# Seven block products in place of eight in the ConvFFN up-projections of a two-layer encoder step

## Chip, cores and metric

The kernel runs on one core of one Trainium2 chip. The metric is the device time of one execution in microseconds. TensorE multiplies, VectorE (DVE) and ScalarE (ACT) do elementwise work, GpSimd (POOL) too, and SyncE (SP) issues most DMAs.

## What is computed

One inference step of a trunk of two layers over 1088 tokens of width 1024 in fp32: 1024 tokens of a prompt and 64 of a sample stream. Layer 0 mixes tokens by pooling, layer 1 by a gated linear recurrence (HGRN2); behind each mixer stands a ConvFFN, which the change is about:

```python
def conv_ffn(h, hist, w_up, cw, cb, w_down):          # h: [L, 1024], D_FF = 2816
    up = jnp.einsum('bld,df->blf', h, w_up)           # [L, 2 * 2816]
    gate_pre, val = jnp.split(up, 2, axis=-1)
    ext = jnp.concatenate([hist, gate_pre], axis=1)
    conv = cb
    for j in range(3):
        conv = conv + cw[j] * ext[:, j:j + L]         # causal, along the tokens
    hid = jax.nn.silu(conv) * val
    y = jnp.einsum('blf,fd->bld', hid, w_down)
    return y, ext[:, -2:]

x += mixer(rmsnorm(x)); x += conv_ffn(rmsnorm(x))     # per layer; a last rmsnorm behind both
```

## The kernel before

Activations lie with features on partitions and tokens along the free axis, in three chunks: chunk 0 and 1 of 384 prompt tokens, chunk 2 of 256 prompt and 64 sample tokens, 320 columns (`CH`, `NCOL`). The residual `x` and the normalised activations stay in SBUF. An fp32 product is made of three fp32r matmuls: each operand is split into a high part and the rest (`hnhi`, `hnlo` for activations, `whi`, `wlo` for weights), and `mm3` (L121-125) adds high x high, high x low and low x high.

Weights are streamed. A unit is 128 x 1024: a DMA on SP brings it as `raw` (L102), ScalarE casts it to `whi` (L103), GpSimd subtracts to `wlo` in two halves (L106). There are six places for units (`NW`); `drop` says which have no more use, and `load_ready` then writes the next loads of `queue`. The pooling weights `pw` are units 0 and 1.

A ConvFFN has 22 feature tiles j in 11 groups of two. `up` (L441) makes for a tile and a chunk the gate `pg` and the value `pv`, each of eight k-tiles x 3 = 24 matmuls; ScalarE copies the gate to `ge` (L466) and starts the convolution (L480), VectorE makes its other two steps (L481, L482), ScalarE the silu (L483), VectorE the product `hr` with the value (L485), and `split` makes `hh` (L128, ScalarE) and `hl` (L129, VectorE). The last two columns of a gate go to the next chunk by small copies on GpSimd (`carry`, L465, L468), those of chunk 2 to an output (`ncv`, L475, L476). `down` (L495) makes for each of eight column blocks d a `dn` of six matmuls per chunk and adds it to `x` (L501).

Ahead of each ConvFFN `norm` makes sums of squares (L260, L261), a transposing matmul `nps` (L272), the root on VectorE, another transposing matmul `nr` (L285), and then scales the eight k-tiles (L300) and splits them.

TensorE's order is written ahead of time: each piece is a `Task`, a generator with a priority and delays (`L_HID`, `N_SUM`, ...) behind other tasks, and `run` takes at each planned time the ready task of the lowest priority; where none is ready in the first 130 us it writes small `fill` matmuls (L178). Up parts have rising priorities from 1000, a `down` has 500, pooling and norms come first. The other engines' order comes from the scheduler. In group 0 and in the last one the chunks are the outer loop, in the others the tiles.

Of the kernel before, what the change touches and what calls it, by code (L numbers as in the profile page):

```python
# [43 lines left out]
NW = 6  # L44
# [12 lines left out]
def trunk_kernel(ctx: ExitStack, tc: tile.TileContext, xtok, xs_tok, hist_tok, xf, par, gmix, pw, winm, ident_in,  # L57
# [24 lines left out]
    queue = []  # L82
    loaded = {}

    def q_add(key, src):
# [4 lines left out]
    def load_ready(most=None):  # L90
        """Loads the next units whose place in the ring is free."""
        while queue and (len(order) < NW or order[-NW] in dead) and (most is None or len(order) < most):
            key, src = queue.pop(0)
            i = len(order)
            order.append(key)
            hi = wp.tile([P, D], F32R, name=f"whi{i}", tag="whi")
            lo = wp.tile([P, D], F32R, name=f"wlo{i}", tag="wlo")
            if i in (1, 3, 5):
                raw = sp.tile([P, D], F32, name=f"raw{i}", tag="raw2")
            else:  # L100
                raw = rawp.tile([P, D], F32, name=f"raw{i}", tag="raw")
            nc.sync.dma_start(raw, src)  # L102
            nc.scalar.copy(hi, raw)  # L103
            for o in range(0, D, D // 2):
                cs = slice(o, o + D // 2)
                nc.gpsimd.tensor_tensor(lo[:, cs], raw[:, cs], hi[:, cs].bitcast(F32), op=ALU.subtract)  # L106
# [803 lines left out]
```

## Time and profile before

| | us |
| --- | --- |
| time, median of 3 runs | 2384.64 |
| lowest, highest | 2383.80, 2385.51 |
| span of the profiled execution | 2382.1 |
| TensorE busy in it | 2329.7 |
| VectorE busy | 1277.3 |
| ScalarE busy | 744.8 |
| GpSimd busy | 668.5 |
| ConvFFN of layer 0, about | 100 to 880 |
| HGRN2, about | 880 to 1560 |
| ConvFFN of layer 1, about | 1560 to 2360 |

The span is that of one profiled execution, from its first to its last instruction. Its own time isn't listed beside it; the runs' times lie 1.7 to 3.4 us above the span, and the median 2.5. A matmul's record lasts longer than the distance to the next one, since they are pipelined; the pace is read from the starts.

### The profile page before, as it was taken

The page shows a single profiled execution, that of the slowest core. Times are in us where ns is not written, and L with a number is a line of the kernel's source. Part 1 is how long each engine was busy: PE and PEld are TensorE (multiplying, and loading weights), DVE is VectorE, ACT ScalarE, POOL GpSimd, SP SyncE. Part 2 cuts the span into 40 slices and gives each one's busy share as a digit, 9 for nine tenths or more (in the row PEclk, how much of TensorE's full clock was granted, in tenths as well). Part 3 has the DMA queues.
Part 4 walks back from the last instruction along what each step waited for, and adds up shares of the span by engine and source line. Part 5 has one row for each costly group of instructions (what it writes and reads, how often), then busy time and mean ns, then how long its engine had stood idle before and what let it go on. Part 6 is the DMA issues. An engine that isn't in the chain of part 4 may idle for free.

```text
span 2382.1 us, 35919 instructions
## 1 busy us (share of the span) xinstructions
PE 2329.7 (98%) x14260; PEld 2286.0 (96%) x14260; DVE 1277.3 (54%) x3242; ACT 744.8 (31%) x1502; POOL 668.5 (28%) x842
## 2 busy tenths in 40 slices
PE   9999999999999989999999999989999999999997
PEld 8999999999999989998998998989999999999997
DVE  6834343344443488677667667774443344443446
ACT  5532222322222353323323323343222322222224
POOL 3232222322232252112112112253232322232324
PEclk8999999999999999999999999999999999999999
DMA  7111111111111110001001001001111111111101
GB/s 242 31 54 41 49 45 45 54 36 45 45 45 45 36 55 27 22 31 54 22 22 55 21 31 49 27 23 52 45 45 45 54 41 40 45 45 45 54 27 77
DMA packets 33811, 111.06 MB, mean 47 GB/s; under 512 B 4061, under 2 KB 8029, under 8 KB 33258
## 3 DMA queue, kind: packets, MB, share of 16 engines
q1 hardware_dynamic: 33582, 108.64, 13.7%
q8 instruction: 112, 1.84, 0.3%
q14 instruction: 57, 0.47, 0.1%
q10 hardware_dynamic: 60, 0.12, 0.0%
HBM read 103.03 MB, written 5.72 MB: 46 GB/s over the span
## 4 chain that ended last, share of the span: by engine, by line
PE 87%; DVE 8%; DMA 1%; ACT 1%; POOL 1%; issue 1%; SPq 0%; DVEq 0%; ACTq 0%; POOLq 0%
PE pg L123 7%; PE pg L125 7%; PE pg L124 7%; PE pv L123 7%; PE pv L124 7%; PE pv L125 7%; PE dn L125 7%; PE dn L124 7%; PE dn L123 7%; PE pj L123 4%; PE pj L124 4%; PE pj L125 4%; PE pl L674 3%; DVE q L665 1%; PE op L123 1%; PE op L124 1%
## 5 line engine op out<-in xcount | busy, mean ns | idle before, releaser
L106 POOL TENSOR_TENSOR wlo<-raw,whi 128x512 fp32r<-128x512 f32 x348 | 474.9, 1381 | 1064.2 <-ACT whi L103 1056.3
L501 DVE TENSOR_TENSOR x<-x,dn 128x384 f32<-128x384 f32 (+1 forms) x528 | 279.8, 531 | 239.0 <-PE dn L125 237.2
L123 PE MATMUL dn<-hh,whi 128*128 128x384 f32 (+1 forms) x1056 | 345.1, 327 | 1.9 <-DVE x L501 1.3
L125 PE MATMUL dn<-hh,wlo 128*128 128x384 f32 (+1 forms) x1056 | 344.5, 326 | 0.7 <-POOL wlo L106 0.7
L124 PE MATMUL dn<-hl,whi 128*128 128x384 f32 (+1 forms) x1056 | 344.6, 326 | 0.6 <-DVE hl L129 0.6
L123 PE MATMUL pv<-hnhi,whi 128*128 128x384 f32 (+1 forms) x1056 | 344.8, 327 | 0.0
L123 PE MATMUL pg<-hnhi,whi 128*128 128x384 f32 (+1 forms) x1056 | 344.7, 326 | 0.0
L124 PE MATMUL pv<-hnlo,whi 128*128 128x384 f32 (+1 forms) x1056 | 344.3, 326 | 0.0
L125 PE MATMUL pg<-hnhi,wlo 128*128 128x384 f32 (+1 forms) x1056 | 344.2, 326 | 0.0
L125 PE MATMUL pv<-hnhi,wlo 128*128 128x384 f32 (+1 forms) x1056 | 344.2, 326 | 0.0
L124 PE MATMUL pg<-hnlo,whi 128*128 128x384 f32 (+1 forms) x1056 | 343.9, 326 | 0.0
L481 DVE SCALAR_TENSOR_TENSOR cv<-ge,prm,cv 128x384 f32<-128x384 f32 x132 | 83.5, 633 | 479.7 <-ACT cv L480 469.4
L103 ACT CAST whi<-raw 128x1024 fp32r<-128x1024 f32 x174 | 182.6, 1049 | 494.1 <-PE dn L124 123.7
L123 PE MATMUL pj<-hnhi,whi 128*128 128x384 f32 (+1 forms) x768 | 269.9, 351 | 0.0
L125 PE MATMUL pj<-hnhi,wlo 128*128 128x384 f32 (+1 forms) x768 | 252.6, 329 | 0.0
L124 PE MATMUL pj<-hnlo,whi 128*128 128x384 f32 (+1 forms) x768 | 252.1, 328 | 0.0
L123 PEld LDWEIGHTS dn<-hh,whi 128*128 128x128 f32 x1056 | 198.2, 188 | 3.7 <-DVE x L501 2.4
L125 PEld LDWEIGHTS dn<-hh,wlo 128*128 128x128 f32 x1056 | 198.2, 188 | 1.1 <-POOL wlo L106 1.1
L124 PEld LDWEIGHTS dn<-hl,whi 128*128 128x128 f32 x1056 | 198.1, 188 | 0.8 <-DVE hl L129 0.8
L123 PEld LDWEIGHTS pv<-hnhi,whi 128*128 128x128 f32 x1056 | 198.4, 188 | 0.1
L123 PEld LDWEIGHTS pg<-hnhi,whi 128*128 128x128 f32 x1056 | 198.2, 188 | 0.1
L124 PEld LDWEIGHTS pv<-hnlo,whi 128*128 128x128 f32 x1056 | 198.4, 188 | 0.0
(238 smaller groups left out, 3792.7 us busy)
## 6 DMA issues: line engine op xcount, KB each, us to landing
raw<-w_up_in SPq DMA_DIRECT2D x88, 512.0 KB, 3.2
raw<-w_dn_in SPq DMA_DIRECT2D x44, 512.0 KB, 3.2
raw<-w_in_in SPq DMA_DIRECT2D x32, 512.0 KB, 3.2
raw<-w_out_in SPq DMA_DIRECT2D x8, 512.0 KB, 3.2
xt<-xtok_in SPq DMA_DIRECT2D x7, 448.0 KB, 6.1
x<-xf_in SPq DMA_DIRECT2D x2, 1536.0 KB, 9.3
y_out<-x SPq DMA_DIRECT2D x8, 384.0 KB, 2.3
x<-xf_in SPq DMA_DIRECT2D x1, 1280.0 KB, 8.2
```

What stands on the lines that cost most here:

```text
L103: nc.scalar.copy(hi, raw)
L106: nc.gpsimd.tensor_tensor(lo[:, cs], raw[:, cs], hi[:, cs].bitcast(F32), op=ALU.subtract)
L123: nc.tensor.matmul(ps, w[0][:, wsl], a_hi, start=first, stop=False)
L124: nc.tensor.matmul(ps, w[0][:, wsl], a_lo, start=False, stop=False)
L125: nc.tensor.matmul(ps, w[1][:, wsl], a_hi, start=False, stop=last)
L481: nc.vector.scalar_tensor_tensor(t[:, :wd], ge[:, 0:wd], prm[:, cw[0]:cw[0] + 1], t[:, :wd], op0=ALU.mult, op1=ALU.add)
L501: nc.vector.tensor_tensor(x[c][:, d, :], x[c][:, d, :], pd[:, :n], op=ALU.add)
L665: nc.vector.tensor_tensor(dst, src, fac, op=ALU.mult)
L674: nc.tensor.matmul(pls[-1][:w, i % 2 * MW:i % 2 * MW + 3 * w // 2], kk[:, o:o + w], mv, start=True, stop=True)
```

## The change

For ten of the eleven groups of each ConvFFN, the gate and value of a feature tile over chunks 0 and 1 are taken as one product of 2 x 2 blocks: the weight blocks a11, a12 (gate, k-tiles 0-3 and 4-7), a21, a22 (value) and the activation blocks b11, b21 (chunk 0, k-tiles 0-3 and 4-7), b12, b22 (chunk 1). Strassen's scheme makes it of seven block products of 12 matmuls instead of eight. Product 1 is (a11+a22)(b11+b22), 2 (a21+a22) b11, 3 a11 (b12-b22), 4 a22 (b21-b11), 5 (a11+a12) b22, 6 (a21-a11)(b11+b12), 7 (a12-a22)(b21+b22). Products 3 and 5 are added up in one bank (`px`, the gate of chunk 1), 4 and 2 in another (`py`, the value of chunk 0); `e` holds 1+3+4, from which the other two results come by VectorE and GpSimd (`part`, L653).

- **Sums of activations.** `sums` (L403) makes the five right-hand sums: sum 1 in a new tile (`mix..1`), sums 4 and 3 in place in `hn` of chunk 0 and chunk 1 (`sum..4k`, `sum..3k`, for k 0-3), 7 and 6 in new tiles. Each of the four k-steps is three VectorE operations (L419, L420, L421), a cast on ScalarE and a subtraction on GpSimd (L169); for 7 and 6 every second L420 is on GpSimd. Group 0 is computed plainly, chunk after chunk, while they are made; sum 4 waits for chunk 0's last use in it and sum 3 for chunk 1's.
- **Weights.** The unit is a half, 128 x 512, in eight places (four more in the HGRN2 part), with five `raw` buffers. `q_mix` (L128) loads a block or, for products 1, 2, 5, 6 and 7, two blocks that VectorE adds or subtracts (L134) ahead of the cast.
- **Order.** A group is: products 3, 4, 1, 5 of its first tile and chunk 2 plainly, the `down` of the group before (chunks inside the column block; `L_HID` 8.5), products 2, 7, 6, then the second tile. In group 1 product 4 stands first. In the last group chunk 2 is computed at the end, from blocks that are loaded again. The plain part starts the convolution behind `pg`, ahead of `pv`.
- The work tiles of norms, HGRN2 and ConvFFN share buffers in another way, and two delays of the norm ahead of HGRN2 are longer.

The instructions on TensorE go from 13538 matmuls to 13079, 66 and 87 of which are `fill`; on VectorE from 3242 to 3714, on GpSimd from 842 to 1138, SP's DMAs from 236 to 818.

```diff
-NW = 6
+NR, NR_G = 8, 4
+NRAW = 5
...
+            hi = pool.tile([P, HW_], F32R, name=f"whi{nm}", tag=f"whi{i}", bufs=1)
+            lo = pool.tile([P, HW_], F32R, name=f"wlo{nm}", tag=f"wlo{i}", bufs=1)
+            src = make(nm)
+            nc.scalar.copy(hi, src)
+            nc.gpsimd.tensor_tensor(lo, src, hi.bitcast(F32), op=ALU.subtract)
...
+    PARTS = {"a11": (0,), "a12": (1,), "a21": (2,), "a22": (3,), "a5": (0, 1, ALU.add), "a2": (2, 3, ALU.add),
+             "a1": (0, 3, ALU.add), "a7": (1, 3, ALU.subtract), "a6": (2, 0, ALU.subtract)}
...
+            t = [raw_block(f"{nm}_{b}", (gate, val)[b // 2], b % 2) for b in bs[:2]]
+            if len(t) > 1:
+                nc.vector.tensor_tensor(t[0], t[0], t[1], op=bs[2])
...
+    def sums(l, ts, after, used=None):
...
+        while used and used.done is None:
+            yield 0.0, 1.0
+        n = [0]
+        for t in ts:
+            op = ALU.subtract if t in "43" else ALU.add
+            (ah, al), (bh, bl) = {"1": (quarter[0], quarter[3]), "4": (quarter[2], quarter[0]), "3": (quarter[1], quarter[3]),
+                                  "7": (mix["4"], mix["1"]), "6": (mix["3"], mix["1"])}[t]
+            for k in range(4):
...
+                with tc.issue_after(after()):
+                    nc.vector.tensor_tensor(m, ah[:, k, :].bitcast(F32), bh[:, k, :].bitcast(F32), op=op)
+                    (nc.gpsimd if t in "76" and k % 2 else nc.vector).tensor_tensor(r, al[:, k, :].bitcast(F32), bl[:, k, :].bitcast(F32), op=op)
+                    nc.vector.tensor_tensor(m, m, r, op=ALU.add)
+                    split(mix[t][0][:, k, :], mix[t][1][:, k, :], m, nc.gpsimd)
+                yield 0.0, L_MIX[t in "76"]
...
+        def prod(ps, key, t, first=True):
...
+            for k in range(4):
+                mm3(ps[:, :N0], get(key), slice(k * P, k * P + P), mix[t][0][:, k, :], mix[t][1][:, k, :], first and k == 0, k == 3, not first)
...
+                if t in "341":
+                    if hasattr(self, "e"):
+                        nc.vector.tensor_tensor(self.e, self.e, ps[:, :N0], op=ALU.add)
+                    else:
+                        self.e = kept(f"e{nm}", "e", 2, ps)
...
+                elif t == "7":
+                    g0 = slot(f"g{nm}", "g", 1)[:, :N0]
+                    nc.gpsimd.tensor_tensor(g0, self.e, self.ge1[:, 2:2 + N0], op=ALU.subtract)
...
+                    nc.gpsimd.tensor_tensor(self.e, self.e, self.v0, op=ALU.subtract)
+                    nc.vector.tensor_tensor(ge0[:, 2:2 + N0], g0, ps[:, :N0], op=ALU.add)
...
+                b0, b1 = (Block(j, jj, hid) for jj, j in enumerate(js))
+                a = task(lambda b=b0, end=end, gi=gi: up_a(b, end, "34"[gi == 1]), prev)
+                Task(lambda f=before: down(*f), 500, [(prev, L_HID), (a, 0.0)])
+                prev = task(lambda b=b0, end=end: up_b(b, end), a)
```

TensorE at the start, layer 0. `pg0_1_0` is the gate of feature tile 1 over chunk 0, `nr_f01` the second transposing matmul of chunk 1's norm. Before:

```order
L124 MATMUL pv0_0_0_668<-hnlo0_103,whi3_297 128x384
L125 MATMUL pv0_0_0_668<-hnhi0_100,wlo3_298 128x384
L123 MATMUL pg0_1_0_775<-hnhi0_100,whi4_304 128x384
L124 MATMUL pg0_1_0_775<-hnlo0_103,whi4_304 128x384
L125 MATMUL pg0_1_0_775<-hnhi0_100,wlo4_305 128x384
L123 MATMUL pg0_1_0_775<-hnhi0_100,whi4_304 128x384
L124 MATMUL pg0_1_0_775<-hnlo0_103,whi4_304 128x384
L125 MATMUL pg0_1_0_775<-hnhi0_100,wlo4_305 128x384
L123 MATMUL pg0_1_0_775<-hnhi0_100,whi4_304 128x384
L124 MATMUL pg0_1_0_775<-hnlo0_103,whi4_304 128x384
L125 MATMUL pg0_1_0_775<-hnhi0_100,wlo4_305 128x384
L285 MATMUL nr_f01_786<-ident_88,nt_f01_700 128x128 x3
```

And now, where `pd2_0` is the first matmul of chunk 2's pooling:

```order
L165 MATMUL pv0_0_0_670<-hnhi0_97,wloup_0_0_a22_315 128x384
L242 MATMUL fill_779<-warm_86 128x128 x2
L242 MATMUL fill_782<-warm_86 128x128 x2
L242 MATMUL fill_785<-warm_86 128x128
L382 MATMUL nr_f01_787<-ident_85,nt_f01_711 128x128 x3
L242 MATMUL fill_795<-warm_86 128x128
L242 MATMUL fill_801<-warm_86 128x128 x2
L242 MATMUL fill_808<-warm_86 128x128 x2
L242 MATMUL fill_815<-warm_86 128x128
L242 MATMUL fill_817<-warm_86 128x128
L242 MATMUL fill_823<-warm_86 128x128
L242 MATMUL fill_825<-warm_86 128x128
```

The matmuls of tile 1 over chunk 0 stood around `nr_f01` and ahead of chunk 2's pooling; now they stand behind chunk 2's pooling mix, and single `fill` matmuls, 21 up to `pd2_0`, are in their place.

GpSimd at the end of group 0 in layer 0: `wlo8` to `wlo10` are low parts of units 8 to 10, two halves each, and `ncv0` the output of the convolution's last columns. Before:

```order
L106 TENSOR_TENSOR wlo8_1370<-raw8_1371,whi8_1369 128x512
L475 COPY ncv0_95<-ge0_0_2_1350 128x2
L476 COPY ncv0_95<-ge0_0_2_1350 128x2
L106 TENSOR_TENSOR wlo8_1370<-raw8_1371,whi8_1369 128x512
L463 MEMSET ge0_2_0_1658 128x2
L106 TENSOR_TENSOR wlo9_1377<-raw9_1378,whi9_1376 128x512 x2
L106 TENSOR_TENSOR wlo10_1517<-raw10_1518,whi10_1516 128x512
L475 COPY ncv0_95<-ge0_1_2_1497 128x2
L476 COPY ncv0_95<-ge0_1_2_1497 128x2
L106 TENSOR_TENSOR wlo10_1517<-raw10_1518,whi10_1516 128x512
```

And now, with `hnlo0` and `hnlo1` the low parts of sums 4 and 3, and `wloup` and `wlodn` those of a weight half of group 1's up and group 0's down part:

```order
L169 TENSOR_TENSOR hnlo0_100<-sum042_1387,hnhi0_97 128x384
L169 TENSOR_TENSOR hnlo0_100<-sum043_1415,hnhi0_97 128x384
L111 TENSOR_TENSOR wloup_0_2_a12_1469<-rawup_0_2_a12_1_1470,whiup_0_2_a12_1468 128x512
L111 TENSOR_TENSOR wloup_0_2_a21_1494<-rawup_0_2_a21_2_1495,whiup_0_2_a21_1493 128x512
L169 TENSOR_TENSOR hnlo1_101<-sum030_1452,hnhi1_98 128x384
L580 COPY ncv0_92<-ge0_1_2_1499 128x2
L581 COPY ncv0_92<-ge0_1_2_1499 128x2
L111 TENSOR_TENSOR wlodn_0_0_0_1531<-rawdn_0_0_0_1532,whidn_0_0_0_1530 128x512
L169 TENSOR_TENSOR hnlo1_101<-sum031_1477,hnhi1_98 128x384
L111 TENSOR_TENSOR wlodn_0_1_0_1556<-rawdn_0_1_0_1557,whidn_0_1_0_1555 128x512
L169 TENSOR_TENSOR hnlo1_101<-sum032_1514,hnhi1_98 128x384
L169 TENSOR_TENSOR hnlo1_101<-sum033_1539,hnhi1_98 128x384
```

Six subtractions for sums stand among those of the weights, and two of down weights among those of sum 3.

## Rows read from the trace of the kernel before

**Rows 1.** The page's first part: busy time of each engine, its share of the span and its instructions.

```profile
PE 2329.7 (98%) x14260; PEld 2286.0 (96%) x14260; DVE 1277.3 (54%) x3242; ACT 744.8 (31%) x1502; POOL 668.5 (28%) x842
```

**Rows 2.** Busy time by stretch (start:end in us): the length, then TensorE's busy time, weight loads, VectorE, ScalarE, GpSimd with their instructions, the granted clock, the DMA engines' share and GB/s. 160:840 and 1640:2320 lie within the ConvFFN of layer 0 and of layer 1.

```profile
60.00:160.00 100.00, 97.51 (x595) 96.45 (x594) 68.21 (x158) 42.47 (x87) 29.60 (x39) 0.97 0.12 38
160.00:840.00 680.00, 680.00 (x4131) 679.96 (x4130) 281.69 (x492) 183.93 (x311) 191.04 (x267) 1.00 0.13 44
840.00:960.00 120.00, 109.78 (x659) 103.97 (x659) 98.94 (x281) 51.20 (x112) 49.68 (x47) 0.96 0.14 45
1500.00:1600.00 100.00, 91.27 (x563) 86.10 (x562) 77.01 (x235) 45.35 (x107) 41.09 (x44) 0.97 0.07 23
1640.00:2320.00 680.00, 680.00 (x4136) 680.00 (x4135) 276.08 (x476) 183.76 (x310) 196.03 (x270) 1.00 0.14 46
```

**Rows 3.** The chain that ended last: its shares of the span by engine.

```profile
PE 87%; DVE 8%; DMA 1%; ACT 1%; POOL 1%; issue 1%; SPq 0%; DVEq 0%; ACTq 0%; POOLq 0%
```

**Rows 4.** TensorE's instructions one by one in a ConvFFN group of layer 0: start, duration, engine, line, operation. First two matmuls of a down part over 320 columns, with 28 more between them left out; then the first of a gate projection over 384 columns and the first of the value projection behind it, with 23 between them left out.

```profile
299.80 0.31 PE L124 MATMUL dn<-hl,whi 128*128 128x320 f32 x1
...
304.05 0.33 PE L123 MATMUL pv<-hnhi,whi 128*128 128x384 f32 x1
...
305.09 0.33 PE L123 MATMUL pg<-hnhi,whi 128*128 128x384 f32 x1
...
309.25 0.33 PE L123 MATMUL pv<-hnhi,whi 128*128 128x384 f32 x1
...
```

**Rows 5.** VectorE's groups of instructions at 160 to 840 us, each shape apart: busy time, mean ns of one, and the idle time ahead of them.

```profile
L501 DVE TENSOR_TENSOR x<-x,dn 128x384 f32<-128x384 f32 x152 | 84.0, 554 | 73.1 <-PE dn L125 72.5
L482 DVE SCALAR_TENSOR_TENSOR cv<-ge,prm,cv 128x384 f32<-128x384 f32 x39 | 41.5, 1063 | 1.3
L501 DVE TENSOR_TENSOR x<-x,dn 128x320 f32<-128x320 f32 x75 | 36.6, 487 | 38.0 <-PE dn L125 38.0
L129 DVE TENSOR_TENSOR hl<-hr,hh 128x384 fp32r<-128x384 f32 x40 | 29.3, 731 | 22.6 <-ACT hh L128 22.6
L481 DVE SCALAR_TENSOR_TENSOR cv<-ge,prm,cv 128x384 f32<-128x384 f32 x39 | 24.1, 618 | 157.4 <-ACT cv L480 157.4
L485 DVE TENSOR_TENSOR hr<-cv,pv 128x384 f32<-128x384 f32 x40 | 22.2, 554 | 23.1 <-PE pv L125 11.8 <-ACT cv L483 11.2
```

**Rows 6.** The same view of the same stretch for GpSimd, and for ScalarE's cast of a weight unit and its copy of a gate.

```profile
L106 POOL TENSOR_TENSOR wlo<-raw,whi 128x512 fp32r<-128x512 f32 x112 | 155.4, 1402 | 363.1 <-ACT whi L103 358.8 <-PE dn L125 4.3
L475 POOL COPY ncv<-ge 128x2 f32<-128x2 f32 x18 | 8.6, 480 | 0.0
L476 POOL COPY ncv<-ge 128x2 f32<-128x2 f32 x18 | 3.2, 180 | 0.0
...
L103 ACT CAST whi<-raw 128x1024 fp32r<-128x1024 f32 x56 | 58.8, 1050 | 186.1 <-PE dn L124 61.9 <-DMA raw<-w_up_in 53.6 <-DMA raw<-w_dn_in 42.4
...
L466 ACT COPY ge<-pg 128x384 f32<-128x384 f32 x39 | 18.6, 477 | 78.5 <-PE pg L125 78.5
```

**Rows 7.** VectorE and GpSimd one by one around 314 us: start, duration, engine, line, operation; x2 is a pair in a row, recorded as one. The last row is a single subtraction of GpSimd, 6 us later.

```profile
313.69 0.62 DVE L481 SCALAR_TENSOR_TENSOR cv<-ge,prm,cv 128x384 f32<-128x384 f32 x1 [5.95 <-ACT cv L480]
314.35 1.53 DVE L482 SCALAR_TENSOR_TENSOR cv<-ge,prm,cv 128x384 f32<-128x384 f32 x1
...
312.55 2.91 POOL L106 TENSOR_TENSOR wlo<-raw,whi 128x512 fp32r<-128x512 f32 x2 [5.23 <-ACT whi L103]
...
320.02 1.30 POOL L106 TENSOR_TENSOR wlo<-raw,whi 128x512 fp32r<-128x512 f32 x1 [3.82 <-ACT whi L103]
```

**Rows 8.** The start: busy time in two stretches (columns as in rows 2), and two of VectorE's groups at 60 to 125 us: the scaling of chunk 2 in the norm ahead of layer 0's ConvFFN, and the sum of squares of a chunk of 384 columns, which reads SBUF with both inputs.

```profile
40.00:80.00 40.00, 36.76 (x249) 35.76 (x248) 37.58 (x95) 27.00 (x50) 15.18 (x15) 1.00 0.30 93
80.00:120.00 40.00, 38.71 (x232) 38.00 (x232) 33.27 (x77) 19.37 (x46) 11.40 (x15) 0.91 0.11 36
...
L300 DVE SCALAR_TENSOR_TENSOR hn_f<-x,prm,nr_f 128x320 f32<-128x320 f32 x8 | 4.2, 537 | 0.0
...
L261 DVE TENSOR_TENSOR acc_f<-acc_f,sq_f 128x384 f32<-128x384 f32 x6 | 3.1, 553 | 0.2
```

**Rows 9.** GpSimd's subtraction of a high part from an activation of 384 columns, at 60 to 160 us.

```profile
L129 POOL TENSOR_TENSOR hnlo<-hn_f,hnhi 128x384 fp32r<-128x384 f32 x5 | 5.3, 1052 | 13.8 <-ACT hnhi L128 13.8
```

**Rows 10.** The page's part on DMA issues, for a unit of up-projection weights: KB each, and us from issue to landing.

```profile
raw<-w_up_in SPq DMA_DIRECT2D x88, 512.0 KB, 3.2
```

**Rows 11.** Busy time in three short stretches at norms (columns as in rows 2); the granted clock is the number behind GpSimd's.

```profile
84.80:91.60 6.80, 6.80 (x31) 6.80 (x30) 2.73 (x10) 2.61 (x11) 1.00 (x1) 0.50 0.19 54
890.30:897.10 6.80, 5.40 (x17) 5.43 (x18) 5.57 (x26) 0.23 (x1) 0.00 (x0) 0.50 0.23 77
1549.00:1556.00 7.00, 4.28 (x13) 3.65 (x14) 5.74 (x14) 2.57 (x5) 5.36 (x5) 0.51 0.24 75
```

**Rows 12.** TensorE's waits: the line, what it waited for, us in total, times, the longest.

```profile
PE dn L123 <- DVE x L501: 1.3, 2, 0.7
PE dn L125 <- POOL wlo L106: 0.7, 1, 0.7
```

More of the change, by code (lines that the diff above doesn't have):

```diff
@@ L83, in trunk_kernel @@
     loaded = {}
-    def q_add(key, src):
-        queue.append((key, src))
-    order, dead = [], set()
+    places = {}
+    free = [(i, False) for i in range(NR)]
     def load_ready(most=None):
[L92 to L106, printed above, removed]
-            loaded[key] = (hi, lo)
+        while queue and (most is None or len(loaded) < most):
+            ph, key, make = queue[0]
+            own = [p for p in free if p[1]] if ph == "g" else []
+            p = own[0] if own else next((p for p in free if not p[1]), None)
+            if p is None:
+                return
+            free.remove(p)
+            queue.pop(0)
+            places[key] = p
+            i, extra = p
+            pool = gp if extra else wp
+            nm = "_".join(str(k) for k in key)
+            hi = pool.tile([P, HW_], F32R, name=f"whi{nm}", tag=f"whi{i}", bufs=1)
[3 more added lines that the diff above has]
+            nc.gpsimd.tensor_tensor(lo, src, hi.bitcast(F32), op=ALU.subtract)
+            loaded[key] = (hi, lo)
@@ L109, in drop, with q_mix, make @@
+    def q_mix(key, gate, val, part):
+        bs = PARTS[part]
+        def make(nm):
+            t = [raw_block(f"{nm}_{b}", (gate, val)[b // 2], b % 2) for b in bs[:2]]
+            if len(t) > 1:
+                nc.vector.tensor_tensor(t[0], t[0], t[1], op=bs[2])
+            return t[0]
+        queue.append(("f", key + (part,), make))
     def drop(*keys):
-        dead.update(keys)
+        for k in keys:
+            p = places.pop(k)
+            if not p[1] or mix["g"]:
+                free.append(p)
@@ L252, in norm @@
         n = NCOL[c]
-        acc = [tmp.tile([P, NMAX], F32, name=f"acc{i}_{nm}", tag=f"acc{i}", bufs=1) for i in range(2)]
+        tags = ("ge", 3, "cv", 3) if kind == 2 else ("e", 2, "v", 2)
+        acc = [slot(f"acc{i}_{nm}", *tags[:2]) for i in range(2)]
         for d in range(ND):
@@ new lines, in ffn @@
+            before = js, (0, 1, 2), hid
+        after, dn = [], prev
+        v0, v1 = (lambda: parts((b0, "6"))), (lambda: parts((b1, "6")))
+        p = task(v1, task(v0, prev))
+        dn_deps = [(prev, L_HID), (p, L_HID)]
+        p = task(lambda: plain(js[1], 1, 2, hid, "p"), task(lambda: plain(js[0], 0, 2, hid, "p"), p))
+        dn_deps.append((p, L_HID))
+        for c in range(3):
+            dn = Task(lambda c=c: down(js, (c,), hid), 500, [(dn, 0.0), dn_deps[c]])
+            after.append(Task(lambda c=c: norm(c, gbase, f"{nm}{c}", kind), c, [(dn, 0.0)], N_END[kind]))
```

359 lines of the change are left out of this document (244 added, 115 removed).

## Prediction

> **What bounds the kernel now.** I read the page's first part, the busy time by stretch, the chain that ended last, and then TensorE's matmuls one by one. TensorE is busy for 98% of the span, VectorE for 54%, GpSimd for 28% [rows 1], and 87% of the chain is TensorE's [rows 3]. In the two ConvFFN stretches TensorE has no idle time at all: 680.00 us busy of 680.00, VectorE 282 and 276, GpSimd 191 and 196 [rows 2]. Its waits for a weight or a residual in down are 0.7 and 1.3 us in the whole run [rows 12]. So a matmul taken out of these stretches saves its pace, as long as no other engine becomes late. A record lasts 0.33 us, but the next one starts before it ends: 24 matmuls of 384 columns start between 305.09 and 309.25, that is 4.16 / 24 = 173.3 ns each; 29 of 320 columns between 299.80 and 304.05 take 146.6 ns each [rows 4].
>
> A group of two feature tiles is then 192 up matmuls of 384 columns, 96 of 320, and in the down part 96 and 48: 288 x 0.1733 + 144 x 0.1466 = 71.0 us. The 680 us hold 9.58 groups; VectorE works 281.69 / 9.58 = 29.4 us in each and GpSimd 19.9.
>
> **A, the products.** A feature tile over chunks 0 and 1 has 96 matmuls; seven products of 12 have 84. With 20 feature tiles per layer and two layers that is 12 x 40 = 480 fewer, all of 384 columns: 480 x 173.3 ns = **-83.2 us**. Nothing else on TensorE shrinks. A group becomes 66.9 us.
>
> **B, the start: +7.** Eight half places hold the four blocks of pooling weights and those of feature tile 0, so tile 1 loads only once chunk 2 has been mixed. Its 48 matmuls over chunk 0, which stood ahead of chunk 2's pooling, move behind it: 48 x 0.1733 = 8.3 us of work leave a place where they covered VectorE's norms and pooling, and single fill matmuls stand there instead. VectorE is the bound there (37.58 of 40 us, then 33.27 of 40 [rows 8]), so the hole stays, less the convolution and hidden product of that tile, 2 x 0.618 + 0.554 + 0.554 = 2.3 us [rows 5], which go with it. Bounds: 3 (half of VectorE's 6.7 us of idle time taken up as well) to 8.3; I take 7, near the upper end, as the stretch's VectorE row is almost full.
>
> **C, the sums before group 1: +29 (16 in layer 0, 13 in layer 1).** In group 0 TensorE runs chunk 1 (96 x 0.1733 = 16.6 us) and chunk 2 (96 x 0.1466 = 14.1), then product 4 (2.1) and product 3, whose last inputs are due 1.6 us later: 34.4 us after chunk 1 began. GpSimd's order up to there is seen in the table of its rows: behind the first freed block (12 x 0.1466 = 1.8 us into chunk 2, at 18.4) and its load and cast, about 3 us more (a unit of twice the size lands in 3.2 us [rows 10]), it has eight weight subtractions of 1.40 [rows 6], eight of sums at 1.05 [rows 9] and four small copies of some 0.33 on the mean [rows 6]: 11.2 + 8.4 + 1.3 = 21 us, so it ends at 42 or later: 8 us late if nothing disturbs it. Two down-weight subtractions stand among sum 3's, though nobody needs them before the down part. VectorE alone gives about the same: it is in chunk 2's norm until about 10 us (eight steps at 0.54 [rows 8] with their low parts), has one tile's convolution by 12.5, then 12 steps of three operations at 0.553, 19.9 us, and the other three convolutions, 7: 39.5, and 1.6 for the last cast and subtraction: 7 late.
>
> The two also hinder each other. One step L481 takes 0.62 us and the L482 behind it, of the same form, takes 1.53, while GpSimd makes its second subtraction, whose pair takes 2.91 where one alone takes 1.30 [rows 7]. L482's mean is 1.063 against 0.618; x += dn, whose one input lies in PSUM, stays at 0.554 [rows 5]. The sums read SBUF with both inputs. If all of it excluded the other engine, the 13.3 us of VectorE's last eight steps would come on top of GpSimd's time: 8 + 13 = 21 late. So layer 0 loses 7 to 21; I take 16, since the nearest row shows the exclusion. In layer 1 all low parts of chunk 2's norm are GpSimd's as well, but sum 1 may start a chunk earlier: 6 to 18, I take 13.
>
> The Trainium skill, "SBUF — State Buffer", section "Who interferes with whom", says that a VectorE instruction with two SBUF inputs and a GpSimd instruction that reads SBUF hold an exclusive lock against each other, and that one SBUF input doesn't contend. By that rule, taken for every pair, C would be 21 + 18 = 39 and the sum 10 us higher; the rows above agree with it at one place, and whether it binds all the time here no row shows.
>
> **D, sums 7 and 6 and the steady groups: +3.** Per group VectorE gains ten weight mixes of 512 columns, 0.69 each (from 0.487 at 320 and 0.554 at 384 columns, 1.05 ns a column), six additions to e and two to ge at 0.554: 29.4 + 6.9 + 4.4 = 40.7 us of 66.9. GpSimd goes from 12 to 22 subtractions and gains four differences of about 1.0: 19.9 + 14.0 + 4 = 38. ScalarE's casts are of half the size and its few copies cost 0.48 each [rows 6]: no bound. A waiting operation is hidden by TensorE's queue: a half weight's place comes free some 12 us before its next content is due in the order, against 3.2 + 0.69 + 0.6 + 1.4 = 6 for load, mix, cast and subtraction; were that cover gone, each late block would cost its own lateness, 22 times a group. The sums 7 and 6, 8 steps or 11 us of VectorE, lie beside the down part. Bounds 0 to 18 (all of them exposed, with half as much again for the lock).
>
> **E, the rest: 0 (-3 to +6).** Down's chunks now alternate within a column block; the matmuls are the same. SP issues 818 DMAs instead of 236, each of half the size; the DMA engines' share in ConvFFN was 0.13-0.14 [rows 2], and twice that has room. The HGRN part keeps its order, with 12 half places for 6 whole ones. The last group runs chunk 2 from reloaded blocks, behind the products, which gives the same work. In three places at norms, where TensorE worked for 4.3 to 6.8 us of some 7, the granted clock was 0.50 to 0.51 (1.2 GHz) [rows 11]: a stall of C may bring such a stretch, up to 3.5 us each, kept for the range.
>
> **Sum.** The profiled execution's span is 2382.1 us; the median of the runs shown is 2384.6, 2.5 more. Span: 2382.1 - 83.2 + 7 + 29 + 3 = 2337.9; on the runs' scale **2340.4 us**. Its own range, from the bounds of B, C and D: 2323 to 2360.
>
> **Rivals.**
> 1. The sums are hidden. My count sets VectorE's twelve steps in one row behind chunk 2's norm; if sum 1 and half of sum 4 fit into gaps ahead of its end, and half of GpSimd's subtractions with them, C is at most 12, D 0 and B 5: 2384.6 - 83.2 + 17 = 2318. For: VectorE works 68 of 100 us at 60 to 160, so there are gaps [rows 2]. Against: GpSimd's 21 us of its own, two weights of which stand ahead of the last sums.
> 2. The exclusion holds for every pair, at the sums and behind them: C 39, D 18, B 7: 2384.6 - 83.2 + 64 = 2365. For: the 1.53 us of that L482 [rows 7]. Against: L481, of the same form, has a mean of 0.618, so most of it passes undisturbed now, at a GpSimd share of 28%.
> 3. Slower: VectorE becomes the bound of every group. It has 32 operations with two SBUF inputs per group (10 mixes, 12 convolution steps, 6 low parts, 4 hidden products from copies). If each waits as long as that L482, 0.91 us [rows 7], it needs 40.7 + 29.1 = 69.8 us where TensorE needs 66.9: 1.2 us a group are left of the 4.16 saved: 2384.6 - 24 + 7 + 39 = 2407. It turns to slower where the mean wait passes (71.0 - 46 / 20 - 40.7) / 32 = 0.88 us. Against: L482 waits 0.45 on the mean, L481 none; at 0.45, VectorE needs 55 of 66.9.
>
> **Chances.** Forecast 0.52, rival 1 0.23, rival 2 0.17, rival 3 0.05, and 0.03 for no change in between. A measurement of this kernel tells about 0.2%, 4.8 us, from none. Faster 0.91, same 0.03, slower 0.06. The range of 2312 to 2372 leaves out rival 3, the far ends of 1 and 2, and no more.
>
> **What would show it.** TensorE's instructions in a steady group should take 66.9 us with no idle time; VectorE should be busy some 41 to 55 us of it, GpSimd 38. At product 3 (px of tile 2) of either layer TensorE should wait 8 to 20 us for hnlo of chunk 1 from GpSimd, with a granted clock of about 0.5 behind it; around chunk 2's pooling there should be single fill matmuls and waits for VectorE. The weight subtractions should have a mean above 1.40 and the mixes one above 0.69. The prediction is wrong if TensorE idles in the steady groups, waiting for weights or e, or if there is no wait at product 3.

## The result, and the profile after

The changed kernel takes 2398.09 us (median of 5 runs, 2395.02 to 2398.61) where the kernel before took 2384.64 beside it: a ratio of 1.0063, with a 95% interval of 1.0046 to 1.0081. The forecast was 2340.4, faster; it is slower by 13.5 us. The profiled span is 2396.8, 14.7 over that of before.

The first line of the page, and the busy time of three stretches (columns as in [rows 2]):

```profile
PE 2293.8 (96%) x13822; PEld 2236.8 (93%) x13822; DVE 1632.1 (68%) x3714; ACT 909.1 (38%) x1964; POOL 1085.7 (45%) x1138
```

```profile
130.00:170.00 40.00, 25.61 (x118) 21.86 (x117) 38.63 (x50) 14.85 (x32) 28.05 (x24) 0.79 0.16 53
160.00:840.00 680.00, 669.51 (x3988) 663.15 (x3989) 432.38 (x690) 255.24 (x495) 382.90 (x407) 0.99 0.38 122
1640.00:2320.00 680.00, 666.59 (x3977) 660.39 (x3977) 440.13 (x698) 253.99 (x494) 387.69 (x405) 0.99 0.38 121
```

The ConvFFN stretches were full before, 680.00 us of 680 [rows 2]; now TensorE is busy for 669.5 and 666.6. At 130 to 170 us, where group 0 of layer 0 ends and the first seven products start, it works 25.6 of 40 us at a mean clock of 0.79, while VectorE works 38.6 of them. What TensorE waits for between 120 and 210 us:

```profile
PE py L163 <- DVE hr L598: 4.8, 1, 4.8
PE px L164 <- POOL hnlo L169: 3.8, 4, 2.1
PE dn L163 <- DVE x L713: 3.5, 3, 2.5
PE pv L163 <- ACT ge L640: 2.4, 1, 2.4
PE px L163 <- ACT ge L640: 1.8, 1, 1.8
PE px L163 <- ACT hnhi L168: 1.4, 1, 1.4
```

The sums' low and high parts (hnlo, hnhi) are late for 5.2 us at product 3; chunk 2's hidden product (`hr`, VectorE) is late for 4.8, gates (`ge`, ScalarE, whose queue waits for VectorE's sums) for 4.2, and x in the down part for 3.5. Behind these waits the granted clock is low; run 7 below asks what that costs.

How long a group takes is read from the start of the last matmul of its down part, in us:

| | before | after | sums left out |
| --- | --- | --- | --- |
| layer 0, end of group 0 | 161.75 | 209.70 | 178.63 |
| a steady group of layer 0 | 71.08 | 67.37 to 69.27 | 67.15 to 68.21 |
| layer 0, end of group 10 | 876.55 | 890.48 | 854.68 |
| from there to layer 1, end of group 0 | 783.26 | 818.17 | 785.10 |
| a steady group of layer 1 | 71.08 | 67.37 to 67.61 | 67.15 to 68.65 |

(Group 0's down part stands later in the new order, so the first row compares the last two kernels only.) A steady group fell by 3.71 us at best, not by the 4.16 of the forecast, but it fell. What the change lost, it lost elsewhere.

### The profile page after: what moved, and what is told of

Read it like the earlier page. It is cut to its first block, busy times and chain, and to the rows that moved or that the text cites. A ratio compares the mean times of both kernels' runs of the same rounds, so it can differ in the third digit from the quotient of the medians.

```text
span 2396.8 us, 38137 instructions
## 1 busy us (share of the span) xinstructions
PE 2293.8 (96%) x13822; PEld 2236.8 (93%) x13822; DVE 1632.1 (68%) x3714; ACT 909.1 (38%) x1964; POOL 1085.7 (45%) x1138
## 5 line engine op out<-in xcount | busy, mean ns | idle before, releaser
L111 POOL TENSOR_TENSOR wloup_a<-rawup_a,whiup_a 128x512 fp32r<-128x512 f32 x368 | 516.0, 1418 | 514.0 <-ACT whiup_a L110 458.4
L110 ACT CAST whiup_a<-rawup_a 128x512 fp32r<-128x512 f32 x368 | 224.5, 618 | 559.1 <-PE dn L164 378.4
L134 DVE TENSOR_TENSOR rawup_a<-rawup_a,rawup_a 128x512 f32<-128x512 f32 x200 | 178.7, 894 | 295.2 <-DMA rawup_a<-w_up_in 280.1
L163 PE MATMUL dn<-hh,whidn 128*128 128x384 f32 (+1 forms) x1056 | 353.6, 335 | 14.3 <-DVE x L713 10.3
L164 PE MATMUL dn<-hl,whidn 128*128 128x384 f32 (+1 forms) x1056 | 350.0, 331 | 0.7 <-DVE hl L169 0.7
L165 PE MATMUL dn<-hh,wlodn 128*128 128x384 f32 (+1 forms) x1056 | 349.5, 331 | 0.0
L713 DVE TENSOR_TENSOR x<-x,dn 128x384 f32<-128x384 f32 (+1 forms) x528 | 261.3, 527 | 89.4 <-PE dn L165 88.2
L163 PE MATMUL pj<-hnhi,whiin 128*128 128x384 f32 (+1 forms) x768 | 269.4, 351 | 1.1 <-ACT hnhi L168 1.1
L164 PE MATMUL pj<-hnlo,whiin 128*128 128x384 f32 (+1 forms) x768 | 252.1, 328 | 2.3 <-POOL hnlo L169 2.3
L165 PE MATMUL pj<-hnhi,wloin 128*128 128x384 f32 (+1 forms) x768 | 252.1, 328 | 0.0
L163 PEld LDWEIGHTS dn<-hh,whidn 128*128 128x128 f32 x1056 | 201.3, 191 | 22.0 <-DVE x L713 18.1
L164 PEld LDWEIGHTS dn<-hl,whidn 128*128 128x128 f32 x1056 | 201.3, 191 | 1.3 <-DVE hl L169 1.3
```

The costliest lines, as they stand in the source:

```text
L110: nc.scalar.copy(hi, src)
L111: nc.gpsimd.tensor_tensor(lo, src, hi.bitcast(F32), op=ALU.subtract)
L134: nc.vector.tensor_tensor(t[0], t[0], t[1], op=bs[2])
L713: nc.vector.tensor_tensor(x[c][:, d, :], x[c][:, d, :], pd[:, :n], op=ALU.add)
```

## The experiments

Theory L: VectorE's operations that read two inputs from SBUF and GpSimd's operations take turns, so that in the stretch of the sums their times add up while TensorE waits. Rival W: VectorE's own amount of work is what is late. Other rivals stand with the runs. All spans are to be held against 2396.8.

How far a span can be read: the changed kernel's five runs span 2393.2 to 2396.8 us, the profiled one is the longest of them, runs 1 to 10 have one execution each, and the kernel before, timed beside them, took 2373.6 to 2386.1 us. So a difference of a few us in a single span shows nothing. Part of it is the start: chunk 1's first matmul in layer 0, ahead of every sum, stands at 110.25 us in the changed kernel's profile, at 107.5 to 109.8 in the other runs and at 101.0 in run 3.

**1. Sums left out.** The body of `sums` is empty, and its three new tiles are quarters of `hn`.

```diff
-                    nc.vector.tensor_tensor(m, ah[:, k, :].bitcast(F32), bh[:, k, :].bitcast(F32), op=op)
... (the other four operations of the step too)
-            mix[t] = tuple(pool.tile([P, 4, NMAX], F32R, name=f"mix{l}{p}{t}") for p in ("h", "l"))
+            mix[t] = quarter["176".index(t)]
```

> The five activation sums are left out (the products read the unsummed blocks); all else stays. The changed kernel loses, against TensorE's matmuls at full pace, 29 us around the first product group of layer 0 and 33 us in layer 1, where the kernel before loses 1.4 and 2.4. Theory L (the sums and GpSimd's subtractions exclude each other while TensorE waits): nearly all of this is the sums', so the span falls from 2396.8 by 50 to 59, to about 2342. Rival W (VectorE's convolutions, weight mixes and the half-size weight loads alone are late there): half or more of the loss stays, 2365 to 2390.

Span 2329.5: the sums cost 67.3 us, more than all that was counted around them, 31.1 up to group 0's end in layer 0 and 33.1 from the end of layer 0 to the same place in layer 1. The stretch of 130 to 170 us in that run:

```profile
130.00:170.00 40.00, 39.97 (x252) 39.65 (x251) 20.08 (x36) 14.20 (x28) 23.08 (x26) 1.00 0.40 128
```

TensorE is full, at full clock, with the weight mixes, the halves and the convolutions all in place. So these alone are not late there in layer 0. The other side of it: without sums the kernel is 52.6 us under the span of before, where A and B were to give 76.2. Some 24 us are lost that have nothing to do with sums.

**2. The sums' low parts on VectorE.**

```diff
-                    split(mix[t][0][:, k, :], mix[t][1][:, k, :], m, nc.gpsimd)
+                    split(mix[t][0][:, k, :], mix[t][1][:, k, :], m, nc.vector)
```

> The last step of each sum, the subtraction to the low part, is done by VectorE instead of GpSimd. VectorE gets 20 operations of 0.54 us more per layer, 12 of them ahead of product 3; GpSimd loses as many of 1.0 to 1.3. Theory L: what counts is the sum of both engines' times, which falls by about 0.5 to 0.7 a step, and a hand-over between them goes: 6 to 10 us less per layer, span 2377 to 2385. Rival W (VectorE's own amount of work bounds): 12 x 0.54 = 6.5 us more per layer, span about 2410.

Span 2376.3, 20.5 less. VectorE got 20 more operations per layer, and the kernel became faster: W, which wanted 13 more, is out as it was put.

**3. One input, first try.** `tensor_scalar(.., 1.0, None, op0=ALU.mult)` in place of the three `tensor_tensor` of a step.

> The three VectorE operations of each sum step keep their tiles and sizes but read one SBUF input instead of two (a multiplication by 1.0; the sum is not formed). Theory L: they no longer exclude GpSimd, and the waits at product 3 fall from 12 us to those of GpSimd's own queue, about 5 to 8, with less time at the low clock: 15 to 20 us less per layer, span about 2361. Rival W: only what the operations themselves become shorter (0.42 instead of 0.55): 36 x 0.13 = 4.7 us per layer, span about 2387.

Span 2370.7, between the two, and the run doesn't tell them apart: the operation was badly chosen. In the trace it takes 0.35 us, or up to 1.45, not the 0.42 expected, and the long ones stand beside GpSimd. First VectorE, then GpSimd in that run (start, duration, line):

```profile
138.00 1.16 DVE L421 TENSOR_SCALAR sum<-sum 128x384 f32<-128x384 f32 x1
139.08 1.43 DVE L420 TENSOR_SCALAR sul<-hnlo 128x384 f32<-128x384 f32 x1
```

```profile
137.76 1.18 POOL L169 TENSOR_TENSOR hnlo<-sum,hnhi 128x384 fp32r<-128x384 f32 x1 [0.84 <-ACT hnhi L168]
138.90 1.39 POOL L111 TENSOR_TENSOR wloup_a<-rawup_a,whiup_a 128x512 fp32r<-128x512 f32 x1
```

So it was shorter, and it still took turns. And 9.3 of its 26.1 us have nothing to do with the sums: chunk 1 began that much earlier, behind a start at another granted clock (third number from the right). The changed kernel, then this run:

```profile
20.00:40.00 20.00, 20.00 (x98) 20.00 (x97) 10.06 (x19) 12.01 (x23) 5.04 (x4) 0.67 0.63 199
```

```profile
20.00:40.00 20.00, 20.00 (x155) 20.00 (x154) 17.33 (x46) 15.57 (x30) 7.56 (x6) 1.00 0.91 278
```

**4. One input, second try.** `tensor_reduce` over an axis of length 1, in the same three places:

```diff
-                    nc.vector.tensor_tensor(m, ah[:, k, :].bitcast(F32), bh[:, k, :].bitcast(F32), op=op)
+                    nc.vector.tensor_reduce(m, ah[:, k, :].bitcast(F32).unsqueeze(2), axis=AX.X, op=ALU.add)
... (L420 and L421 likewise)
```

> As the run whose sum steps read one SBUF input (span 2370.7), but by another operation: that multiplication took 0.35 us undisturbed instead of 0.55, and in GpSimd's presence 1.0 to 1.4, so it was shorter and excluded GpSimd all the same. Here each of the three is a tensor_reduce over an axis of length 1 (384 elements read, 384 written, one input; the sum is not formed), expected at about 0.55 us as the original. Theory L, with the exclusion only for operations that use a second SBUF read: the sum steps and GpSimd's subtractions no longer hinder each other, the operations keep 0.55 us, and the stage falls by 12 to 20 us per layer: span 2357 to 2372. Rival W (the number and length of VectorE's operations): span 2392 to 2397. If the tensor_reduce waits for GpSimd as well, its mean is near 0.9 and the span stays above 2390.

Span 2366.4, 30.4 less, with as many operations of the same undisturbed length; four of them per layer, in sums 7 and 6, went from GpSimd to VectorE with the edit. VectorE's groups in the sums of layer 0, at 120 to 168 us, in the changed kernel and in this run (mean ns behind the busy time):

```profile
L421 DVE TENSOR_TENSOR sum<-sum,sul 128x384 f32<-128x384 f32 x13 | 13.0, 1004 | 0.1
L420 DVE TENSOR_TENSOR sul<-hnlo 128x384 f32<-128x384 f32 x8 | 7.2, 904 | 0.1
L419 DVE TENSOR_TENSOR sum<-hnhi 128x384 f32<-128x384 f32 x8 | 5.2, 649 | 0.9 <-POOL hnlo L169 0.9
```

```profile
L420 DVE TENSOR_REDUCE sul<-hnlo 128x384 f32<-128x384 f32 x20 | 10.8, 542 | 0.1
L419 DVE TENSOR_REDUCE sum<-hnhi 128x384 f32<-128x384 f32 x17 | 9.2, 545 | 2.5 <-POOL hnlo L169 2.5
L421 DVE TENSOR_REDUCE sum<-sum 128x384 f32<-128x384 f32 x16 | 8.7, 541 | 0.0
L587 DVE SCALAR_TENSOR_TENSOR cv<-ge,prm,cv 128x322 f32<-128x322 f32 x3 | 3.0, 999 | 0.0
```

L421 takes 1004 ns on the mean with two inputs and 541 with one; the convolution's steps, which still read two, stay near 1000. GpSimd's subtraction of a weight half falls from 1579 to 1391 ns, of a sum from 1205 to 1075:

```profile
L169 POOL TENSOR_TENSOR hnlo<-sum,hnhi 128x384 fp32r<-128x384 f32 x8 | 9.6, 1205 | 6.7 <-ACT hnhi L168 6.7
L111 POOL TENSOR_TENSOR wloup_a<-rawup_a,whiup_a 128x512 fp32r<-128x512 f32 x6 | 9.4, 1579 | 0.0
```

```profile
L111 POOL TENSOR_TENSOR wloup_a<-rawup_a,whiup_a 128x512 fp32r<-128x512 f32 x9 | 12.5, 1391 | 0.0
...
L169 POOL TENSOR_TENSOR hnlo<-sum,hnhi 128x384 fp32r<-128x384 f32 x8 | 8.6, 1075 | 1.4 <-ACT hnhi L168 1.4
```

This is the run that shows theory L most directly: the operations' length and number kept, the second SBUF input gone. The four operations per layer that left GpSimd, about 1 us each, are a second difference, and too small for 30 us. TensorE's only waits at 120 to 210 us are then 4.9 us for hnlo at product 3, which is GpSimd's own queue.

**5. The weights' low parts on VectorE as well,** on top of run 2, for the 13 halves per layer around the sums:

```diff
+            own = key[:1] + key[2:3] in (("up", 2), ("dn", 0), ("dn", 1))
-            nc.gpsimd.tensor_tensor(lo, src, hi.bitcast(F32), op=ALU.subtract)
+            (nc.vector if own else nc.gpsimd).tensor_tensor(lo, src, hi.bitcast(F32), op=ALU.subtract)
```

> As the run in which VectorE makes the low parts of the sums (span 2376.3), and VectorE also makes the low parts of the 13 weight halves per layer that are loaded around the sums (feature tile 2's and group 0's down weights), 8 of which are ahead of product 3. GpSimd then has only small copies in that stage. Theory L: a subtraction of 512 columns takes 0.69 us on VectorE against 1.3 to 1.6 on GpSimd, which VectorE had to wait out: 3 to 6 us less per layer, span 2364 to 2371. Rival W (VectorE's own amount of work): 8 x 0.69 = 5.5 us more per layer, span about 2387.

Span 2367.6, 8.7 less than run 2; from the same start, group 0's end came 7.4 us earlier in layer 0, and the way from layer 0's next to last group to group 0's end in layer 1 fell by 4.5. Moving more work on the busier engine paid a second time.

**6. Only sums 7 and 6 left out.**

```diff
+                if t in "76":
+                    mixed.add((l, t))
+                    continue
```

> Only sums 7 and 6 are left out (their products read unsummed blocks); sums 1, 4 and 3 are made as before. All five sums cost 67 us in span. If term D of the prediction was of the right size (sums 7 and 6 cost 3 us in all), the span falls to about 2394. If they cost as theory L has it, 8 steps per layer whose operations take turns with GpSimd beside VectorE's 24 additions to x, the waits for x in down (3.5 us per layer) and some 4 to 8 us behind product 3 go: span 2378 to 2386.

Span 2380.6: they cost 16.2 us where term D had 3. Sums 1, 4 and 3 are then the other 51.1, where C had 29.

These are differences of whole spans. From chunk 1's first matmul to the last of group 0's down part alone, all five sums cost 28.5 us in layer 0 (99.45 against 70.93 in run 1) and 28.8 in layer 1 (103.25 against 74.48). In run 6 the two stretches take 92.42 and 96.96, so sums 7 and 6 cost 7.0 and 6.3 there, and sums 1, 4 and 3 cost 21.5 and 22.5. The other 10 us of the 67.3 lie outside: 2.6 ahead of the first sum, 9.0 between the two stretches, and 1.6 less behind the second.

**7. Fills in the stall.** Is the low clock a cost of its own?

```diff
             for k in range(4):
+                if t in "43" and key[2] == 2:
+                    fill(((2.6, 0.9, 0.9, 0.9), (1.2, 1.8, 1.8, 1.8))[t == "3"][k])
```

> Small fill matmuls, 5.3 + 6.6 us of them per layer at the fill's planned 0.22 us, are set ahead of the k-steps of products 4 and 3 of the first product group, where TensorE waits; nothing else changes. If the low granted clock behind the waits (0.51 to 0.67 there) costs time of its own, products 4, 3 and 1 run at 173 ns a matmul instead of 290 to 310, and the span falls by 4 to 8 us per layer, to 2381 to 2389. If the waits for the sums' inputs alone set the end, the span stays at 2397 or rises by 1 to 3.

Span 2397.5: no gain. The clock was kept ahead of product 5, as the first two of three stretches of the changed kernel and of this run show (the number behind GpSimd's is the granted clock):

```profile
150.00:160.00 10.00, 5.57 (x17) 4.08 (x16) 9.97 (x11) 3.91 (x9) 8.96 (x9) 0.67 0.20 65
160.00:170.00 10.00, 7.32 (x20) 5.55 (x21) 9.72 (x16) 2.75 (x6) 5.91 (x5) 0.51 0.12 43
170.00:180.00 10.00, 10.00 (x67) 10.00 (x67) 4.70 (x6) 4.73 (x10) 9.05 (x11) 1.00 0.33 105
```

```profile
150.00:160.00 10.00, 9.79 (x74) 9.16 (x73) 9.97 (x13) 4.08 (x9) 7.92 (x8) 1.00 0.29 85
160.00:170.00 10.00, 5.12 (x34) 4.72 (x33) 9.32 (x13) 2.89 (x7) 6.41 (x6) 1.00 0.15 47
170.00:180.00 10.00, 8.37 (x37) 8.37 (x38) 4.42 (x6) 2.04 (x4) 6.75 (x9) 0.66 0.28 91
```

0.67 and 0.51 became 1.00 and 1.00, and product 1 ran at 173 ns a matmul. But then product 5 waits 5.7 us, and runs at the low clock in its turn:

```profile
PE px L163 <- DVE e L671: 5.7, 1, 5.7
```

It waits until VectorE has added product 3 to e. In the changed kernel that addition came right behind product 3, and product 5 didn't wait; in this run it stands behind five operations of sums 7 and 6 and two weight mixes:

```profile
166.80 0.55 DVE L669 TENSOR_TENSOR e<-e,px 128x384 f32<-128x384 f32 x1 [0.28 <-PE px L165]
```

```profile
171.03 0.55 DVE L671 TENSOR_TENSOR e<-e,px 128x384 f32<-128x384 f32 x1
```

So the edit changed VectorE's order too, and the run doesn't settle what the low clock costs by itself. From chunk 1's first matmul to group 0's end in layer 0 it takes 102.0 us where the changed kernel takes 99.5: a kept clock alone brought nothing, while VectorE's queue set the end.

**8. One block per weight.** Products 1, 2, 5, 6 and 7 take one loaded block, so 200 mixes and 200 loads are left out.

```diff
-            t = [raw_block(f"{nm}_{b}", (gate, val)[b // 2], b % 2) for b in bs[:2]]
+            t = [raw_block(f"{nm}_{b}", (gate, val)[b // 2], b % 2) for b in bs[:1]]
```

> Each weight of products 1, 2, 5, 6, 7 is loaded from one block instead of two, so VectorE's 200 weight mixes and 200 of the 818 loads are left out; the products use the unmixed blocks. Theory L (VectorE's two-input operations and GpSimd's work exclude each other): the steady groups have cover, so they stay at about 67.3 us, without the single ones of 68 to 69; the sums' stage gets only the three mixes in it freed, 2 to 5 us per layer. Span 2375 to 2388. Rival M (the mixes and their traffic are what the change loses): the groups fall to 66.9 us, the stage and the ends by 10 us per layer, span below 2365.

Span 2378.1. Every steady group now takes 67.37 to 67.40 us, none 68 or 69, and none 66.9: the pace isn't the mixes', the single longer groups are. Such a one in the changed kernel, VectorE and then TensorE (in brackets the idle time ahead and what ended it):

```profile
458.68 0.22 DVE L598 TENSOR_TENSOR hr<-cv,pv 128x64 f32<-128x64 f32 x1
462.10 0.69 DVE L134 TENSOR_TENSOR rawup_a<-rawup_a,rawup_a 128x512 f32<-128x512 f32 x1 [3.21 <-DMA rawup_a<-w_up_in]
462.71 1.41 DVE L713 TENSOR_TENSOR x<-x,dn 128x384 f32<-128x384 f32 x3
```

```profile
463.32 0.41 PE L163 MATMUL dn<-hh,whidn 128*128 128x320 f32 x1 [1.52 <-DVE x L713]
```

The mix L134 stands at the head of VectorE's queue and waits 3.21 us for its load; the additions to x behind it (L713) wait with it, the banks stay full, and the down part stops for 1.52 us. The cover that I counted, 12 us from a free place to its use, is TensorE's; VectorE's queue has none.

**9. Sums by TensorE.** Sums 1, 4 and 3 are four matmuls with an identity, or its negative, into PSUM; ScalarE casts from there, and VectorE subtracts with one input in PSUM.

```diff
+                    for w_, a_ in ((idr, ah), (idr, al), (sg, bh), (sg, bl)):
+                        nc.tensor.matmul(ps, w_, a_[:, k, :], start=a_ is ah, stop=a_ is bl)
+                    nc.scalar.copy(mix[t][0][:, k, :], ps)
+                    nc.vector.tensor_tensor(mix[t][1][:, k, :], ps, mix[t][0][:, k, :].bitcast(F32), op=ALU.subtract)
```

> Sums 1, 4 and 3 are formed by TensorE in PSUM: four matmuls of 384 columns with an identity or its negative per step, then ScalarE's cast and one VectorE subtraction with one PSUM input. TensorE gets 12 x 4 x 0.173 = 8.3 us more per layer, VectorE loses 12 x 1.1 us, GpSimd 12 subtractions. Theory L: the stall in front of product 3 goes, 25 us less waiting and low clock per layer against 8.3 us of work: span about 2363. Rival W: VectorE's 13 us less against 8.3 more: span about 2387.

Span 2376.8, 20.0 less, and between the two: no wait at product 3 was left, but 7.3 us of waits of product 5 for e, behind sums 7 and 6, and 3.8 for the identity in layer 1, whose place is free only when HGRN2's tiles are.

**10 to 12. A version that beats both.** Run 10 also starts sum 1 of layer 1 with sum 4, sums 7 and 6 9 us later, and gives their low parts to VectorE; run 11 starts them after 4 us in layer 1; run 12 adds the edit of run 5.

```diff
-                    t = Task(lambda: sums(l, "1", lambda: hn_ready[1].value), 3, [(hn_ready[1], 0.0)] + late_deps)
-                    t = Task(lambda: sums(l, "4", late, last_of[0]), 3, [(t, 0.0), (hn_ready[2], 0.0)])
+                t = Task(lambda: sums(l, "14", late, last_of[0]), 3, [(hn_ready[2], 0.0)])
...
-                Task(lambda: sums(l, "76", late), 3, [(t, 0.0)])
+                Task(lambda: sums(l, "76", late), 3, [(t, 9.0)])               # run 10
+                Task(lambda: sums(l, "76", late), 3, [(t, 4.0 if l else 9.0)]) # runs 11 and 12
```

> As the run with sums 1, 4 and 3 formed by TensorE (span 2376.8), with three more edits: in layer 1 sum 1 starts with sum 4, as in layer 0, so that TensorE no longer waits 3.8 us for the place of the identity; sums 7 and 6 start 9 us later, so that VectorE's addition of product 3 to e isn't behind them (product 5 waits for it 4.2 and 3.1 us, and the clock is low behind that); and their low parts are VectorE's. Theory L: these 11 us and the low clock go: span 2358 to 2366. Rival W: VectorE's 8 more operations per layer make it late in the down part, 2372 to 2380.

Span 2361.0, as L had it; but group 1 of layer 1 took 75.44 us, since product 6 waited 3.7 us for its sum.

> As the run with TensorE's sums and late sums 7 and 6 (span 2361.0), but in layer 1 sums 7 and 6 start 4 us after sum 3 instead of 9, since product 6 waited 3.7 us for them there and ran at a low clock behind that. Theory L: this 8 us (group 1 of layer 1 took 75.4 us) goes for the most part: span 2353 to 2357, time 2355 to 2359, 1.1 to 1.3% faster than the kernel before. If the earlier start makes product 5 wait for VectorE's addition to e again, the span stays at 2358 to 2363.

Time 2362.02 (6 runs), 0.9926 of before (0.9909 to 0.9942). That group fell to 67.42, but the span stayed, at 2361.9: 3.1 us were lost between layer 0's end and group 0's end in layer 1, and the rest in single groups of 68 to 69, which wait for x, like the one shown at run 8, or for e. The first part of that is not explained. The expected 2353 to 2357 was missed.

> As the tuned run with TensorE's sums (span 2361.9, time 2362.0), and VectorE makes the low parts of the 13 weight halves per layer around the sums, as in the run that fell by 8.7 us so. With sums 1, 4 and 3 on TensorE little of VectorE's two-input work is left in that stage, so theory L gives a smaller gain: 0 to 4 us, time 2357 to 2362. Rival W: VectorE's 9 us more per layer make it late for x in the down part, time 2364 to 2372.

Time 2355.62 (4 runs), 0.9891 of before (0.9869 to 0.9914): the fastest here, and better than expected. Between 120 and 210 us TensorE has no wait left in that run. It is 1.1% faster than the kernel before, with Strassen's products kept.

## Why the prediction was wrong, step by step

Against the span of before, in us. A stretch's loss is its length less its matmuls at their undisturbed pace (173.3 and 146.6 ns from [rows 4], 112 ns for a fill), taken for the run without sums beside the kernel before.

| term | forecast | measured | from |
| --- | --- | --- | --- |
| A, products | -83.2 | -83.2 of work | 480 matmuls fewer |
| B, start | +7 | +8.8 | 21 more fills, recorded as two of 0.112 each, and 4.1 more loss up to group 0's end |
| C, sums 1, 4, 3 | +29 | +51.1 | runs 1 and 6 |
| D, sums 7, 6 | +3 | +16.2 | run 6 |
| D, steady groups | 0 | +15.7 | losses of 7.8 and 9.1 up to the last group, before 0.7 and 0.5 |
| E, ends and HGRN2 | 0 | +6.0 | layer 0's end +10.0, HGRN2 with the start of layer 1 -12.5, tail +8.5 |
| sum | -44.2 | +14.6 | span: +14.7 |

- **What bounds the kernel, and A,** were right: TensorE's pace set the steady groups before and after.
- **B** was right in kind and nearly in size: fills and waits for VectorE stand around chunk 2's pooling.
- **C is the single term that failed most,** 29 against 51.1, of which 44 lie within the sums' stretches (run 6). The mechanism was named, and L is shown by run 4; its size was taken too small. For layer 0 I took 16 us out of 7 to 21, as if more than a third of the exclusion were hidden. Chunk 1's matmuls began at 110.2 us and sum 3's last low part was made at 165.7, 55.5 us later and 21 later than the 34.4 that I had as due, and sums 1, 4 and 3 cost 21.5 us there: the upper bound was the plain value. The 4.83 us that product 4 waited for chunk 2's hidden product, which stood in the same queue, are part of these 21 and not beside them. The nearest row was [rows 7], one pair of operations in a stretch where GpSimd worked 28% of the time; at the sums it was near 70% (28.05 of 40 us), and 13 of the 36 operations of these sums took 1.0 to 1.6 us instead of 0.55, which is 11 us.
- **C in layer 1** came out at 22.5, above the upper bound of 18. I had counted the early start of sum 1 as a gain of 3. It was a loss: VectorE had sum 1 ahead of chunk 2's sums of squares, and TensorE's transposing matmul `nps` waited 4.0 us for these, which it doesn't do in run 1, nor in run 10, where sum 1 starts later. Two of TensorE's waits at 1590 to 1715 us in the changed kernel:

```profile
PE nps_f L369 <- DVE acc_f L364: 4.0, 1, 4.0
PE dn L163 <- DVE x L713: 3.9, 3, 2.7
```

- **Rival 2's C,** the exclusion for every pair, was 39, ten more than I took, and it was the better end. The Trainium skill, "SBUF — State Buffer", section "Who interferes with whom", also lets a one-input operation that uses both ports hinder GpSimd, which I left out when I read it; run 3's 0.35 and up to 1.45 us agree with that, run 4's 0.54 with its statement that a tensor_reduce never does.
- **D failed twice,** 3 against 32 for its two rows. Sums 7 and 6 weren't hidden by the down part, since the additions to x share VectorE with them: the down part waits 3.5 and 3.9 us for x, and in run 6 not at all. Its bound of 18 was also worked out for the 8 steps of one layer, and there are 16 (11 us with half as much again is 16.5 for one layer). And the steady groups, which I called covered, lose in three ways: by a pace of 67.15 us instead of 66.9 even without sums, by single waits behind VectorE's mixes, and in the group ahead of the last, which takes 63.9 to 64.4 us and only 61.5 in run 8.
- **E** was taken as zero; the tail lost 8.5. Layer 0's end and HGRN2 border on each other and some of HGRN2's matmuls move from one to the other, so only their sum, -2.5, says something. No run was made on either, and the causes stay open.
- **Rival 2** came nearest: C, D and B of 64 against 76 measured; what it lacked is steady groups and ends. Rival 3's mechanism, VectorE as the bound of every group, didn't happen: 432 us of 680 in layer 0. The forecast's own range, 2323 to 2360, is narrower than the bounds of B, C and D added up, 2317 to 2367, and neither holds the result. The sign turned because B to E were all too small, and D and E had been taken at or near the favourable end. Two of the forecast's signs came as it had them, VectorE at 42.8 us a group and GpSimd at 37.9 (432.38 and 382.90 of 680): the amounts of work were right, what they do to each other was not.

## What to carry to other kernels

Where two engines exclude each other, add their times over the whole stretch, and charge the backlog to everyone behind it in the queue, as here the norm of chunk 2 and the additions to x, not only to the wait one is looking at; a mean from a stretch in which one of them is mostly idle says nothing of that. Work may be moved on the busier engine and still make the kernel faster, if it is shorter there and the other engine's share of the turns goes. Sums that stand in front of TensorE's work can be made by TensorE itself: 48 matmuls of 0.173 us per layer cost less than the 12 steps that they replaced.

## What the runs showed of the hardware

- VectorE's `tensor_scalar` of 128 x 384 fp32 from SBUF to SBUF took 0.35 us undisturbed and up to 1.45 beside GpSimd's subtractions, though it reads one input; a `tensor_reduce` that reads and writes as many elements took 0.54 in every place (mean 541 to 545 ns over 53).
- A stall with fills in it kept the granted clock at 1.00 where it had been 0.51 to 0.67 (1.2 GHz for part of the time). Behind the next wait, without fills, it was 0.66 where it had been 1.00, and the span rose by 0.7 us.
- Of the same start, three profiles show granted clocks of 0.67, 0.73 and 1.00 at 20 to 40 us (the changed kernel, run 1 and run 3); with 1.00, chunk 1 began 9.3 and 6.7 us earlier than in the first two.
- From 250 to 700 us, the matmuls into `pz` that read the new sum tiles start 176.7 ns apart on the mean (mostly 174 or 179), and in run 1, where they read quarters of `hn`, 173.3. Those of the down part over 384 columns, whose chunks now alternate, start 175.7 ns apart, against 173.6 before. With 72 and 96 of them, a group takes 67.37 us instead of 66.9. The cause of either stays open.
